# A two-layer decoder in float32: blocks of the retention stage between the products of the last projection, and accumulators that start from the residual

## Chip, cores, metric

One NeuronCore of a Trainium2 chip runs the whole program. The metric is the device time of one execution in microseconds (us); the number given for a kernel is the median of several executions. The engines are named as in the profile: PE is TensorE (matrix products), PEld its weight loads, DVE is VectorE, ACT is ScalarE, POOL is GpSimd, and SP is the engine that issues most of the transfers (DMAs). SPq and ACTq are the DMA queues of SP and ACT.

## The reference, cut to what matters

```python
h = concatenate([meta, x])                       # 16 + 1024 tokens, D_MODEL = 1024
h = h + mixer_rglru_swa(rmsnorm(h))              # layer 0
h = h + swiglu(rmsnorm(h))                       # (silu(h @ w_gate) * (h @ w_up)) @ w_down, D_FF = 2816
q, k, v, g = split(rmsnorm(h) @ w_in)            # layer 1: 4 heads, q and k 256 wide, v 512
for chunk in chunks_of_128(q, k, v):             # state: 256 x 512 per head
    qk = (qn @ kn.T) * decay_intra
    o = qk @ vn + (qn * decay_q) @ state
    state = decay_chunk * state + (kn * decay_k).T @ vn
h = h + (silu(g) * rmsnorm(o)) @ w_out
h = h + swiglu(rmsnorm(h))
return h[16:]                                    # everything in float32
```

## The kernel before, in words

Features lie on the partitions and tokens on the free axis, in two halves (`hf`). The stream `h` is eight tiles by two halves, `h[m][hf]`. A float32 product is three products of split operands (`mm3`, lines 160 to 162): each operand is written as a rounded part and a rest (`hi` and `lo` for a weight, `oh` and `ol` for an operand that moves). The rounded part is a cast on ACT (L111, L790), the rest a subtraction on DVE or POOL (L113, L791). The large products are done two tiles by two with seven products in place of eight: `unit22` loads four weight tiles and forms their sums and differences S1 to S4 on POOL (L145, L146, L149, L151), and `seven` runs the products in the order of `PRODUCTS` into two PSUM tags of four banks (`ps`, `ax`). After each product `evac` takes the result out of PSUM: a copy on ACT where a block of the output is met for the first time, else an add on DVE.

**The down projection of the FFN** (`ffn`, one per layer) goes over groups of two or three pairs of hidden tiles: `DG` has (2, 3, 2, 2, 2) pairs in layer 0 and (2, 3, 3, 3) in layer 1. The hidden tiles lie in DRAM (`hd`). Each group loads them again (seven tiles per pair, in `xslot`), splits them (`hilo` into `slot`), and runs four units `mp`, each of which adds into `h[2mp]` and `h[2mp+1]`. In group 0 the first product of a block writes a new tile `h` (ACT, L929), later products add (DVE, L840). The residual lies in DRAM too (`kept`): `residual(m)` loads two tiles after a unit of group 2 or 3 and adds them to `h[m]` on DVE (L910).

**The retention stage** follows the projections `proj7`. The last one, `proj7(15)`, is the gate's. Four heads have nine blocks each, `seq` is their list, and `turn(i)` runs block i: `updates` (six products for the state), `ahead(i + 2)` (load and split of the values with `values`, scores and key transposes with `first`), `outputs` (nine products) and `state` (DVE adds, ACT casts, DVE rests). `third` transposes a block's output and multiplies it with the gate `sg`, which `load_gates` fetches. When four blocks are through, their share of the output projection is put in `fills`, eight closures of twelve products, and `fill(n)` runs n of them. The blocks 0 to 2 of the first head are written ahead of `proj7(15)`; the rest of the loop opens a pool (`rp`) that takes over the memory of the projection's. The reloads of `h` stand in the turns 3 to 10.

The order on each engine is set by a scheduler: it takes the program's order as a priority and lets an instruction pass another one on the same engine when it expects the other to wait. Tiles come from pools: `slot` has 56 buffers, `xslot` 18, and a tile is handed out in the order of the program, when an earlier one is released. Each engine, and each DMA queue, then works strictly in its order.

## Time and profile before

| | |
|---|---|
| median of 3 executions | 2687.58 us (2685.81 to 2689.57) |
| the profiled execution: time, span | 2692.58 us, 2690.8 us |
| PE busy | 2583.9 us, 96% |
| DVE, ACT, POOL busy | 1828.1 us, 1157.2 us, 1454.5 us |
| mean granted clock of TensorE | 0.982 of full speed |
| DMA | 302.32 MB, mean 112 GB/s |

The span is the profiled execution from the first to the last instruction; its time lies 1.8 us above the span. A busy share near 100% of PE does not say that it runs at its peak: the ends of matmuls are modelled, and the granted clock has two levels, so a stretch with fewer matmuls per microsecond than its neighbours has lost time in either way.

### The profile page before, as it was taken

What the parts mean: (1) busy time and instruction counts of PE and PEld (TensorE: products, weight loads), DVE (VectorE), ACT (ScalarE), POOL (GpSimd) and SP (SyncE); (2) the same over time, 40 slices, a digit from 0 to 9 for tenths busy, and PEclk for the clock granted to TensorE, in tenths of its full rate; (3) what the DMA queues carried; (4) which work ended last, traced back from release to release, by engine and by line L of the source; (5) the groups of instructions that cost most, each with busy time, mean ns of one, the idle gap of its engine ahead of it and who ended that gap; (6) DMA issues with size and microseconds to landing.
All of it is one profiled execution on the core that took longest, in us unless ns stands there. A gap on an engine that the chain in (4) does not pass through costs nothing. (4 is left out here: it accounts for less than half of the span.)

```text
span 2690.8 us, 43341 instructions
## 1 busy us (share of the span) xinstructions
PE 2583.9 (96%) x15782; PEld 2289.4 (85%) x15782; DVE 1828.1 (68%) x3119; ACT 1157.2 (43%) x2452; POOL 1454.5 (54%) x1323
## 2 busy tenths in 40 slices
PE   8989999999999998999999998999999999998998
PEld 7878889999999898888999976777778888886776
DVE  6976677566666788987864434566688555556776
ACT  4665543333333533442233345555543333334542
POOL 4746143554554676456765444455555556544774
PEclk9998999999999999999999998999999999999999
DMA  4001152223223543332223234433332322323653
GB/s 153 30 27 37 55 177 78 96 96 112 91 96 135 186 155 108 118 118 103 95 101 98 96 126 160 147 112 126 127 128 90 111 99 98 106 98 118 208 170 112
DMA packets 145318, 302.32 MB, mean 112 GB/s; under 512 B 18512, under 2 KB 35408, under 8 KB 145104
## 3 DMA queue, kind: packets, MB, share of 16 engines
q1 hardware_dynamic: 103792, 232.49, 25.9%
q10 hardware_dynamic: 41152, 66.54, 6.6%
q8 instruction: 124, 2.03, 0.3%
q14 instruction: 90, 0.74, 0.1%
q0 software_dynamic: 160, 0.52, 0.1%
HBM read 216.60 MB, written 82.89 MB: 111 GB/s over the span
## 5 line engine op out<-in xcount | busy, mean ns | idle before, releaser
L160 PE MATMUL ps<-oh,hi 128*128 128x260 f32 (+1 forms) x2160 | 694.7, 324 | 25.9 <-DVE h L840 9.3
L161 PE MATMUL ps<-ol,hi 128*128 128x260 f32 (+1 forms) x2160 | 694.4, 322 | 5.1 <-POOL ol L791 2.8
L162 PE MATMUL ps<-oh,lo 128*128 128x260 f32 (+1 forms) x2160 | 691.4, 323 | 6.1 <-DVE lo L113 6.0
L160 PE MATMUL ax<-oh,hi 128*128 128x260 f32 (+1 forms) x1668 | 535.4, 323 | 5.4 <-DVE h L840 4.8
L161 PE MATMUL ax<-ol,hi 128*128 128x260 f32 (+1 forms) x1668 | 537.2, 323 | 2.3 <-DVE ol L791 1.6
L162 PE MATMUL ax<-oh,lo 128*128 128x260 f32 (+1 forms) x1668 | 532.8, 322 | 1.1 <-DVE lo L113 1.1
L113 DVE TENSOR_TENSOR lo<-S,hi 128x512 fp32r<-128x512 f32 (+2 forms) x380 | 332.5, 876 | 197.4 <-ACT hi L111 183.4
L160 PEld LDWEIGHTS ps<-oh,hi 128*128 128x128 f32 x2160 | 409.5, 190 | 65.1 <-DVE h L840 10.0
L162 PEld LDWEIGHTS ps<-oh,lo 128*128 128x128 f32 x2160 | 409.2, 190 | 41.6 <-DVE lo L113 9.5
L161 PEld LDWEIGHTS ps<-ol,hi 128*128 128x128 f32 x2160 | 410.8, 190 | 39.6 <-POOL ol L791 4.1
L111 ACT CAST hi<-S 128x512 fp32r<-128x512 f32 (+2 forms) x380 | 211.5, 559 | 526.8 <-PE ps L161 245.3
L160 PEld LDWEIGHTS ax<-oh,hi 128*128 128x128 f32 x1668 | 315.8, 190 | 32.0 <-DVE h L840 2.7
L161 PEld LDWEIGHTS ax<-ol,hi 128*128 128x128 f32 x1668 | 315.9, 189 | 28.8 <-DVE ol L791 2.7
L162 PEld LDWEIGHTS ax<-oh,lo 128*128 128x128 f32 x1668 | 314.3, 189 | 27.1 <-DVE lo L113 2.2
L299 POOL TENSOR_TENSOR t<-t,rf 128x520 f32<-128x520 f32 (+1 forms) x181 | 267.1, 1483 | 113.8 <-DVE t L1061 49.5
L111 ACT CAST hi<-raw 128x512 fp32r<-128x512 f32 (+2 forms) x350 | 202.6, 585 | 284.6 <-PE ps L161 142.4
L113 DVE TENSOR_TENSOR lo<-raw,hi 128x512 fp32r<-128x512 f32 (+2 forms) x318 | 258.0, 814 | 97.7 <-ACT hi L111 91.9
L145 POOL TENSOR_TENSOR S<-rb 128x512 f32<-128x512 f32 (+2 forms) x95 | 112.4, 1183 | 341.5 <-DVE lo L113 318.4
L791 POOL TENSOR_TENSOR ol<-raw,oh 128x520 fp32r<-128x520 f32 (+1 forms) x126 | 189.0, 1527 | 26.8 <-ACT oh L790 13.4
L151 POOL TENSOR_TENSOR S<-raw,S 128x512 f32<-128x512 f32 (+2 forms) x95 | 128.1, 1348 | 78.7 <-DVE lo L113 76.0
L146 POOL TENSOR_TENSOR S<-S,raw 128x512 f32<-128x512 f32 (+2 forms) x95 | 113.7, 1197 | 87.4 <-issue 46.3
L149 POOL TENSOR_TENSOR S<-raw,rb 128x512 f32<-128x512 f32 (+2 forms) x95 | 120.6, 1270 | 53.1 <-DVE lo L113 53.1
(306 smaller groups left out, 4812.3 us busy)
## 6 DMA issues: line engine op xcount, KB each, us to landing
raw<-in_wgu_dram SPq DMA_DIRECT2D x50, 512.0 KB, 3.3
raw<-hd SPq DMA_DIRECT2D x77, 260.0 KB, 4.3
raw<-hd SPq DMA_DIRECT2D x77, 256.0 KB, 3.4
rb<-in_wgu_dram SPq DMA_DIRECT2D x38, 512.0 KB, 3.2
raw<-in_wro_dram SPq DMA_DIRECT2D x32, 512.0 KB, 3.3
raw<-in_wr_dram SPq DMA_DIRECT2D x27, 512.0 KB, 3.3
hd<-T ACTq DMA_DIRECT2D x44, 260.0 KB, 2.6
hd<-T ACTq DMA_DIRECT2D x44, 256.0 KB, 3.9
```

The source lines that it names most:

```text
L111: nc.scalar.copy(hi, src)
L113: eng.tensor_tensor(out=lo, in0=src, in1=f32(hi), op=ALU.subtract)
L145: nc.gpsimd.tensor_tensor(out=s1, in0=a21, in1=a22, op=ALU.add)
L146: nc.gpsimd.tensor_tensor(out=s2, in0=s1, in1=a11, op=ALU.subtract)
L149: nc.gpsimd.tensor_tensor(out=s3, in0=a11, in1=a21, op=ALU.subtract)
L151: nc.gpsimd.tensor_tensor(out=s4, in0=a12, in1=s2, op=ALU.subtract)
L160: nc.tensor.matmul(ps, ah, bh, start=first and i == 0, stop=False, skip_group_check=more)
L161: nc.tensor.matmul(ps, ah, bl, start=False, stop=False, skip_group_check=more)
L162: nc.tensor.matmul(ps, al, bh, start=False, stop=last and i == n - 1, skip_group_check=more)
L299: (eng or nc.vector).tensor_tensor(out=out_, in0=a, in1=b, op=ALU.mult)
L791: eng.tensor_tensor(out=lo, in0=src, in1=f32(hi), op=ALU.subtract)
```

## The change

Four things are changed. `seven` takes hooks that run after a product. `proj7(15)` is called with hooks: after its first product the head of the sequence (`begin`), after the next six the turns 0 to 5; its temporaries come from `slot` rather than `aslot`. The values of a block are fetched three turns ahead (`fetch`) and no longer in `values`; the reloads of `h` are issued in the turns 3, 4, 6 and 7, four at a time, and `third` and `fill` are redistributed over the turns 6 to 9. In `ffn`, `preload` loads the residual into the tiles `h` of the units 1 to 3 ahead of their unit, so that all their products add on DVE and neither the copies on ACT nor a later residual add are left; the unit 0 keeps them (`residual(0)`, `residual(1)` in group 2). The rests of group 1's first pair go from DVE to POOL.

```diff
@@ -791,7 +791,7 @@
         eng.tensor_tensor(out=lo, in0=src, in1=f32(hi), op=ALU.subtract)
         return hi, lo
 
-    def seven(u, xs, chunks, evac):
+    def seven(u, xs, chunks, evac, hooks={}):
 
         bk = {}
         n = len(xs)
@@ -805,6 +805,8 @@
                                          xterm(x[xn_], a, b))], new and j == 0, j == n - 1,
                         not new)
             evac(i, [ps[:, :b - a] for ps, (a, b) in zip(bk[t], chunks)])
+            if i in hooks:
+                hooks[i]()
 
     def eight(u, xs, chunks, evac, hooks={}):
 
@@ -909,30 +911,39 @@
                 t = unspill(m, hf, n)
                 nc.vector.tensor_tensor(out=h[m][hf][:, :n], in0=h[m][hf][:, :n], in1=t[:, :n], op=ALU.add)
 
+        def preload(mp):
+            for m in (2 * mp, 2 * mp + 1):
+                for hf in range(2):
+                    h[m][hf] = unspill(m, hf, n, xslot if hf and m >= 4 else None)
+
         for gi, grp in enumerate(groups):
             xs = [{} for _ in grp]
             for ki, key in enumerate(MOVING):
                 for j, i in enumerate(grp):
                     raw = xslot("raw")[:, :n]
                     nc.sync.dma_start(raw, hd[i][key])
-                    xs[j][key] = hilo(raw, n, slot, nc.gpsimd if gi > 1 or j else nc.vector)
+                    xs[j][key] = hilo(raw, n, slot, nc.gpsimd if gi or j else nc.vector)
                 if gi == 0 and ki == 2:
                     keep()
+                if gi == 0 and ki == 4:
+                    preload(1)
             w = len(grp) * P
             for mp in range(4):
+                if gi == 0 and mp in (1, 2):
+                    preload(mp + 1)
                 at = [(2 * mp + r, c) for r, c in ((0, 0), (0, 0), (0, 1), (1, 1), (1, 1), (0, 1), (1, 0))]
 
                 def evac(k, bk):
                     m, hf = at[k]
-                    if gi == 0 and k in (0, 2, 3, 6):
+                    if gi == 0 and mp == 0 and k in (0, 2, 3, 6):
                         h[m][hf] = xslot("h") if hf and m >= 4 else slot("h")
                         each(lambda o, ps: nc.scalar.copy(o, ps), h[m][hf], bk)
                     else:
                         each(add, h[m][hf], bk, h[m][hf])
 
                 seven(unit22(wd[gi][mp], w, fp), xs, chunks, evac)
-                if gi in (2, 3):
-                    residual(4 * gi - 8 + mp)
+                if gi == 2 and mp in (1, 2):
+                    residual(mp - 1)
                 if gi == len(groups) - 1:
                     done(2 * mp)
                     done(2 * mp + 1)
@@ -1043,7 +1054,7 @@
             while pend:
                 pend.pop(0)()
 
-        def proj7(i, chunks, fin):
+        def proj7(i, chunks, fin, hooks={}):
             t = {}
 
             def evac(k, bk):
@@ -1064,7 +1075,7 @@
                 for f in held:
                     f()
 
-            seven(unit22(wr[i], 512, ap), xo2, chunks, evac)
+            seven(unit22(wr[i], 512, ap), xo2, chunks, evac, hooks)
 
         def scaled(chunks, c, t, bk):
             lo, hi = chunks[0][0], chunks[-1][1]
@@ -1185,6 +1196,7 @@
 
         def start(hd):
             k = Head()
+            k.raw = {}
             k.hd, k.kf, k.qf, k.kd, k.on, k.V, k.sp, k.ys, k.am, k.U, k.sg = hd, {}, {}, {}, {}, {}, {}, {}, {}, {}, {}
             return k
 
@@ -1201,11 +1213,20 @@
                     nc.sync.dma_start(k.kf[1][d][:, :512], k1[:, 8:520])
                     nc.sync.dma_start(k.qf[1][d][:, :512], q1)
 
+        def fetch(i):
+
+            if i >= len(seq):
+                return
+            k, b = seq[i]
+            if b in (0, 5):
+                load(k, b // 5)
+            k.raw = {b: slot("vr")[:, :512], **k.raw}
+            for p in range(2):
+                nc.sync.dma_start(k.raw[b][:block(b)[2], p * 256:(p + 1) * 256], vdr[k.hd][b][p])
+
         def values(k, b):
             bn = block(b)[2]
-            raw = slot("vr")[:, :512]
-            for p in range(2):
-                nc.sync.dma_start(raw[:bn, p * 256:(p + 1) * 256], vdr[k.hd][b][p])
+            raw = k.raw.pop(b)
             vh, vl = slot("vh", F32R)[:, :512], slot("vl", F32R)[:, :512]
             nc.scalar.copy(vh[:bn], raw[:bn])
             nc.gpsimd.tensor_tensor(out=vl[:bn], in0=raw[:bn], in1=f32(vh[:bn]), op=ALU.subtract)
@@ -1305,13 +1326,12 @@
 
             if i < len(seq):
                 k, b = seq[i]
-                if b in (0, 5):
-                    load(k, b // 5)
                 values(k, b)
                 first(k, b)
 
         def turn(i):
             k, b = seq[i]
+            fetch(i + 3)
             if b < 8:
                 updates(k, b)
             ahead(i + 2)
@@ -1320,12 +1340,24 @@
             if b < 8:
                 state(k, b)
 
-        ahead(0)
-        ahead(1)
+        def reload(ms, hf):
+            for m in ms:
+                h[m][hf] = unspill(m, hf, 512, rslot if hf else None)
+
+        def begin():
+            ahead(0)
+            ahead(1)
+
+        def hook(i):
+            def run():
+                turn(i)
+                if i in (3, 4):
+                    reload(range(4 * i - 12, 4 * i - 8), 0)
+            return run
+
         for i in range(3):
-            turn(i)
-        temps[0] = aslot
-        proj7(15, REST, gate(7))
+            fetch(i)
+        proj7(15, REST, gate(7), {0: begin, **{i + 1: hook(i) for i in range(6)}})
         while late_:
             late_.pop(0)()
 
@@ -1373,22 +1405,20 @@
             return [(lambda m=m: output(k.hd, hf, m, *k.ys[hf])) for m in range(KD)]
 
         for i, (k, b) in enumerate(seq):
-            if i > 2:
+            if i > 5:
                 turn(i)
-            if 3 <= i < 11:
-                for m in (2 * i - 6, 2 * i - 5):
-                    hf = m // KD
-                    h[m % KD][hf] = unspill(m % KD, hf, 512, rslot if hf else None)
+            if i in (6, 7):
+                reload(range(4 * i - 24, 4 * i - 20), 1)
             if b == 0:
-                fill(1)
-            for k_, b_ in seq[1:4] if i == 4 else seq[i - 1:i] if i > 4 else ():
+                fill(2 if i == 9 else 1)
+            for k_, b_ in {6: seq[1:3], 7: seq[3:5], 8: seq[5:8]}.get(i, seq[i - 1:i]) if i > 5 else ():
                 if not b_:
                     continue
                 third(k_, b_)
                 if b_ in (4, 8):
                     fills += outs(k_, b_ // 8)
             if i not in (32, 33, 34):
-                fill(1 if b in (0, 4, 5) else 2)
+                fill(3 if i < 9 else 1 if b in (0, 4, 5) else 2)
         fill(2)
         third(*seq[-1])
         fill(len(fills))
```

**SP, layer 0, behind the loads of group 0's hidden tiles.** `raw<-hd` is a hidden tile's load, `raw` and `rb<-in_wd` are a unit's weights, `h<-keep` is a residual's load. Before:

```order
L917 DMA raw_10703<-hd_6123 128x520
L141 DMA rb_11006<-in_wd_0_dram 128x512
L140 DMA raw_11153<-in_wd_0_dram 128x512
L141 DMA rb_11154<-in_wd_0_dram 128x512
L140 DMA raw_11427<-in_wd_1_dram 128x768
L141 DMA rb_11428<-in_wd_1_dram 128x768
L140 DMA raw_11613<-in_wd_1_dram 128x768
L141 DMA rb_11614<-in_wd_1_dram 128x768
L917 DMA raw_11301<-hd_6611 128x520
L140 DMA raw_11799<-in_wd_1_dram 128x768
```

and now:

```order
L924 DMA raw_10711<-hd_6123 128x520
L760 DMA h_10867<-keep_1913_4854 128x520
L760 DMA h_10871<-keep_1924_4901 128x520
L760 DMA h_11019<-keep_1935_4948 128x520
L760 DMA h_11023<-keep_1946_4995 128x520
L924 DMA raw_11313<-hd_6611 128x520
L924 DMA raw_11319<-hd_7111 128x520
L924 DMA raw_11325<-hd_7611 128x520
L924 DMA raw_11331<-hd_6613 128x520
L924 DMA raw_11337<-hd_7113 128x520
L141 DMA rb_11026<-in_wd_0_dram 128x512
```

The loads of group 1 (`hd_6611` is its first) stood behind the weights of group 1's second unit; now they stand ahead of the second half of the weights of group 0's unit 2, with the four residual loads of the units 2 and 3 ahead of them.

**POOL, the same place.** The rests of the hidden tiles are `ol<-raw,oh`; 128x256 sums belong to group 0, 128x384 ones to group 1. Before:

```order
L151 TENSOR_TENSOR S_11012<-raw_11005,S_11010 128x256
L151 TENSOR_TENSOR S_11160<-raw_11153,S_11158 128x256
L151 TENSOR_TENSOR S_11434<-raw_11427,S_11432 128x384
L145 TENSOR_TENSOR S_11617<-rb_11614 128x384
L146 TENSOR_TENSOR S_11618<-S_11617,raw_11613 128x384
L149 TENSOR_TENSOR S_11619<-raw_11613,rb_11614 128x384
L791 TENSOR_TENSOR ol_11310<-raw_11307,oh_11309 128x520
L151 TENSOR_TENSOR S_11620<-raw_11613,S_11618 128x384
```

and now:

```order
L151 TENSOR_TENSOR S_11032<-raw_11025,S_11030 128x256
L791 TENSOR_TENSOR ol_11316<-raw_11313,oh_11315 128x520
L145 TENSOR_TENSOR S_11173<-rb_11170 128x256
L791 TENSOR_TENSOR ol_11322<-raw_11319,oh_11321 128x520
L791 TENSOR_TENSOR ol_11328<-raw_11325,oh_11327 128x520
L791 TENSOR_TENSOR ol_11334<-raw_11331,oh_11333 128x520
L146 TENSOR_TENSOR S_11174<-S_11173,raw_11169 128x256
L791 TENSOR_TENSOR ol_11340<-raw_11337,oh_11339 128x520
L791 TENSOR_TENSOR ol_11346<-raw_11343,oh_11345 128x520
L791 TENSOR_TENSOR ol_11352<-raw_11349,oh_11351 128x520
L149 TENSOR_TENSOR S_11175<-raw_11169,rb_11170 128x256
L791 TENSOR_TENSOR ol_11358<-raw_11355,oh_11357 128x520
```

Seven rests of group 1 stand between the sums of group 0's last unit, where none stood, and all 21 of the group are now POOL's and stand ahead of the second sum (L146) of the group's second unit; before, POOL had 14 of the 21, one of them ahead of the second unit's last sum and 13 behind it.

**PE, the start of the first head.** `oh` and `ol` mark products of the projection, `kf` and `qf` the first transposes and scores of a block, `vh` and `kd` the update of the state. Before:

```order
L162 MATMUL ps_19484<-oh_14951,lo_19482 128x512
L1239 MATMUL ax_19612<-ckt,kf_19595 16x128
L1226 MATMUL ax_19625<-qf_19597,kf_19595 128x128
L1239 MATMUL ax_19638<-ckt,kf_19595 128x128
L1239 MATMUL ax_19638<-ckt,kf_19596 128x128
L1239 MATMUL ax_19612<-ckt,kf_19596 16x128
L1226 MATMUL ax_19625<-qf_19598,kf_19596 128x128
L160 MATMUL ax_19644<-vh_19608,kd_19615 128x512
L160 MATMUL ax_19648<-vh_19608,kd_19615 128x512
```

and now:

```order
L162 MATMUL ps_19460<-oh_14927,lo_19458 128x512
L1260 MATMUL ax_19651<-ckt,kf_19571 16x128
L1247 MATMUL ax_19661<-qf_19573,kf_19571 128x128
L1260 MATMUL ax_19674<-ckt,kf_19571 128x128
L160 MATMUL ax_19680<-oh_13770,hi_19602 128x512
...
L162 MATMUL ax_19680<-oh_14334,lo_19604 128x512
L1260 MATMUL ax_19674<-ckt,kf_19572 128x128
L1260 MATMUL ax_19651<-ckt,kf_19572 16x128
L1247 MATMUL ax_19661<-qf_19574,kf_19572 128x128
L160 MATMUL ps_19630<-oh_14691,hi_19608 128x512
...
L162 MATMUL ps_19630<-oh_14915,lo_19610 128x512
L160 MATMUL ax_19698<-vh_19647,kd_19654 128x512
```

Two of the last projection's products, twelve rows each (`ax_19680`, `ps_19630`), now stand between the first transposes and the first update, and its first product further ahead; before, the update came right behind the scores, and all seven products after it.

## Rows read from the trace of the kernel before

**Rows 1.** The page: busy time per engine (share of the span, instructions).

```profile
PE 2583.9 (96%) x15782; PEld 2289.4 (85%) x15782; DVE 1828.1 (68%) x3119; ACT 1157.2 (43%) x2452; POOL 1454.5 (54%) x1323
```

**Rows 2.** Stretches: length, busy us and instructions per engine, granted clock, DMA, GB/s.

```profile
1600.00:1720.00 120.00, 102.28 (x444) 80.64 (x443) 59.56 (x106) 61.17 (x136) 54.73 (x64) 0.91 0.46 155
1720.00:1840.00 120.00, 116.57 (x553) 93.98 (x552) 72.41 (x134) 64.51 (x147) 58.20 (x74) 1.00 0.39 132
910.00:930.00 20.00, 16.22 (x117) 14.40 (x116) 17.21 (x26) 14.26 (x27) 18.28 (x13) 1.00 1.00 356
930.00:985.00 55.00, 55.00 (x461) 55.00 (x460) 44.46 (x81) 23.74 (x47) 40.74 (x33) 1.00 0.53 164
985.00:1010.00 25.00, 21.84 (x152) 20.90 (x151) 24.22 (x45) 6.40 (x17) 20.80 (x19) 0.86 0.53 172
1030.00:1050.00 20.00, 12.77 (x72) 11.46 (x72) 18.50 (x30) 4.50 (x11) 14.41 (x12) 0.74 0.33 110
2480.00:2510.00 30.00, 25.48 (x91) 18.22 (x89) 19.26 (x26) 17.18 (x35) 19.20 (x16) 0.89 0.70 243
2520.00:2575.00 55.00, 55.00 (x239) 44.52 (x238) 39.84 (x55) 24.67 (x47) 45.33 (x35) 1.00 0.53 166
2575.00:2655.00 80.00, 74.83 (x312) 58.99 (x311) 67.32 (x86) 29.10 (x56) 61.86 (x46) 0.98 0.46 145
```

**Rows 3.** PE in order of time: start, length, what; in brackets idle time before, releaser.

```profile
1618.87 0.39 PE L162 MATMUL ps<-oh,lo 128*128 128x512 f32 x1
...
1626.89 1.30 PE L160 MATMUL ax<-vh,kd 16*128 16x512 f32 x2 [3.93 <-ACT kd L1243]
...
1669.70 1.47 PE L1293 MATMUL ax<-ckt,on 128*128 128x128 f32 x12
...
1692.50 0.62 PE L160 MATMUL ps<-yh,hi 128*128 128x512 f32 x1
```

**Rows 4.** SP's queue, 1587 to 1668 us, in order of time: start, length, what.

```profile
1657.84 8.21 SPq L122 DMA_DIRECT2D raw<-in_wro_dram  x2
...
1667.09 1.00 SPq L1208 DMA_DIRECT2D vr<-vd  x2
```

**Rows 5.** Waits of ACT, 1600 to 1720 us.

```profile
ACT vh L1210 <- DMA vr<-vd: 13.5, 4, 5.2
```

**Rows 6.** SP's queue in order of time, the loads of group 1 in either layer.

```profile
908.84 12.82 SPq L917 DMA_DIRECT2D raw<-hd  x19
...
2489.21 16.23 SPq L917 DMA_DIRECT2D raw<-hd  x21
```

**Rows 7.** ACT in order of time; in brackets its idle time before, and its releaser.

```profile
996.13 0.62 ACT L790 CAST oh<-raw 128x520 fp32r<-128x520 f32 x1 [6.71 <-DVE h L910]
...
1038.00 0.62 ACT L790 CAST oh<-raw 128x520 fp32r<-128x520 f32 x1 [5.29 <-DVE h L910]
```

**Rows 8.** Groups by line and shape: count, busy us, mean ns, idle before.

```profile
L791 POOL TENSOR_TENSOR ol<-raw,oh 128x520 fp32r<-128x520 f32 x63 | 93.9, 1515 | 8.9 <-PE ps L161 3.3 <-ACT oh L790 2.4 <-DVE h L840 2.3
L840 DVE TENSOR_TENSOR h<-ps,h 128x260 f32<-128x260 f32 x136 | 53.8, 419 | 15.2 <-PE ps L162 14.8
L910 DVE TENSOR_TENSOR h<-h,h 128x520 f32<-128x520 f32 x16 | 19.8, 1240 | 1.1 <-DMA h<-keep 1.1
L791 POOL TENSOR_TENSOR ol<-T,oh 128x520 fp32r<-128x520 f32 x8 | 16.8, 2106 | 26.4 <-ACT oh L790 26.4
```

**Rows 9.** POOL and ACT in order of time: last sums and last copies of group 0.

```profile
884.78 0.74 POOL L151 TENSOR_TENSOR S<-raw,S 128x256 f32<-128x256 f32 x1 [1.41 <-DVE lo L113]
...
912.47 0.38 ACT L929 COPY h<-ps 128x260 f32<-128x260 f32 x1 [0.28 <-PE ps L162]
...
2474.93 0.74 POOL L151 TENSOR_TENSOR S<-raw,S 128x256 f32<-128x256 f32 x1 [0.89 <-DVE lo L113]
...
2496.49 0.58 ACT L929 COPY h<-ps 128x512 f32<-128x512 f32 x1
```

**Rows 10.** DVE, the last instruction of the program.

```profile
2686.85 0.69 DVE L910 TENSOR_TENSOR h<-h,h 128x512 f32<-128x512 f32 x1
```

## The prediction, made before the run

> **What bounds the kernel now.** I read the page first. PE is busy for 2583.9 us, 96% of the span [rows 1], so work on another engine costs time only where PE waits for it or runs at the lower clock. Next I cut the span into stretches and looked for those with too few matmuls. The reader is to compare neighbours of one kind [rows 2]. In layer 0's down projection PE runs 461 matmuls in the 55 us from 930 on, 8.38 per us. From 910 to 930 it runs 117, worth 14.0 us, so 6.0 us are lost; from 985 to 1010 152, 6.9 lost; from 1030 to 1050 72, 11.4 lost: together 24.3 us. In layer 1 the clean stretch has 239 in 55 us, 4.35 per us; from 2480 to 2510 91 are worth 20.9 us, 9.1 lost; from 2575 to 2655 312 are worth 71.8, 8.2 lost: together 17.3 us. Around the start of the retention heads matmuls have several sizes, so I take idle time and clock: from 1600 to 1720 PE is idle for 17.7 us, and 102.3 busy us at a granted clock of 0.91 miss 9.2 us; the next 120 us, the same work in its steady state, miss 3.4. That is an excess of 23.5 us. The change touches these three places; together they have lost 65 us.
>
> Then I asked each place why. **The heads.** PE's matmuls of the last projection end at 1618.9, and the next large ones start at 1626.9, after a wait for a key tile (`kd`) of ACT's [rows 3]; the four blocks from 1669.7 to 1692.5 are as thin. ACT, which makes the key tiles, waits 13.5 us for values (`vr`) [rows 5], and key tiles queue behind that wait. The values are late since SP issues them late: those at 1667 right behind weight loads that SP held for 8.2 us [rows 4]. **The down projections, group 0 to group 1.** The hidden tiles of group 1 are issued from 908.8 and 2489.2 on [rows 6], when group 0 is almost over. Tiles of `xslot` are handed out in program order, and the last accumulators `h` of group 0 stand ahead of these loads. **Groups 2 and 3.** ACT stands for 6.7 and 5.3 us ahead of a cast whose buffer an L910 add holds [rows 7], and the casts of the next weights queue behind it.
>
> **The change, part by part.** *The residual as a start.* 24 of the 32 adds of L910 go, six pairs in either layer. An L910 of 520 columns takes 1240 ns, a PSUM add of 260 columns 419 ns [rows 8]. In place of 12 L910 per layer (14.9 us of DVE in layer 0) DVE gets 24 PSUM adds of 260 (10.1 us) which ACT's copies were. On paper that is little; what counts is the place: they go from groups 2 and 3, where DVE is at 24.2 of 25 and 18.5 of 20 us [rows 2], to group 0. The Trainium skill, "SBUF — State Buffer", section "Who interferes with whom", says why the one is dear: a DVE instruction with two SBUF inputs contends with GpSimd, one with at most one does not; the trace agrees, 1240 ns for twice the columns of a 419 ns add.
>
> With ACT's block gone I let 5 of the 6.9 us and 7 of the 11.4 us come back: not all, since POOL's bunches of splits between the sums stay, and the four remaining L910 now stand in group 2. Bounds: 0 and 18.3. In layer 1, 2575 to 2655, 4 of 8.2 (0 to 8.2). The end of the program was an L910 behind the last PSUM add [rows 10]; it falls away: 0.7 us, certain.
>
> *Group 1 earlier.* The twelve loads of the residual per layer are 3.2 MB; at the 356 GB/s of [rows 2] 9 us of DMA time, spread over group 0, in which DMA has room; by itself it costs nothing unless a weight comes late behind it. The gain is that splits of group 1 can start 40 us earlier, as far as `slot` has room: 56 buffers less 28 for group 0's operands and 12 accumulators leave 16, eight splits. But all 21 splits now run on POOL, at 1515 ns [rows 8]: 31.8 us, against 21.2 for 14 before. Layer 0: POOL is free at 885.5 [rows 9]; PE wants the last split at the seventh product of group 1's first unit: group 0's last block is copied out at 912.5 [rows 9], and six products of 18 matmuls at 8.38 per us are 12.9 us, so at 925.4, 39.9 us later. Demand: 31.8 and nine sums of 0.74 (256 columns) to about 1.0 us (384), 8: 39.8. Just met on paper; I leave 3 us of waiting in place of 6.0 and book 3 (bounds -6 and 6). Layer 1: free at 2475.7, wanted at 2496.5 [rows 9] + 6 x 9/4.35 = 2508.9, 33.2 us later; demand 31.8 and five sums, 36.8: 3.6 late, and more where the clock falls for it. Of 9.1 us I book 3 (bounds -6 and 9).
>
> A rule speaks against this edit. A rest takes POOL 1515 ns [rows 8], and seven more per layer load it with 10.6 us. The Trainium skill, "GPSIMD Engine Reference", section "Engine selection", wants elementwise work with two inputs on VectorE, GpSimd being about 2 times slower. By the rule alone, with POOL as the only engine that PE waits for at this crossing, all 10.6 would appear in either layer, and the sum would lose 21 us; the earlier start is what the rule leaves out.
>
> *Blocks between products.* No instruction of weight is added. Before, PE had nothing from 1618.9 to 1626.9 [rows 3] but a few transposes and scores. Now a product of 12 matmuls, 12/4.35 = 2.8 us, stands ahead of these and two stand behind: 8.3 us of cover for a hole of 8.0, after which the clock was low for a while. I book 9 for the two (bounds 5 and 10). What is next: the products run out by the fourth block, and blocks 3 to 8 then run without cover. A block has 15 large matmuls, 15/4.35 = 3.4 us, and some small ones: I take 4 us of PE. The values come one block earlier than before, but the `sg` loads and the twelve reloads of `h` share SP with them: from the first reload to the fourth `sg` there are about 5.9 MB, at 356 GB/s 16.6 us, and `third` needs all four. I leave 10 us of loss here and in the start together: 23.5 - 10 = 13.5 gained (bounds -5 and 20).
>
> *The later heads.* Values are fetched three turns ahead rather than two. The stretch from 1720 misses 3.4 us only [rows 2]: nothing booked, 0 to 3.
>
> **The sum.** 5 + 7 + 4 + 0.7 + 3 + 3 + 13.5 = 36.2 us. The profiled execution took 2692.6 us, so 2656.4 for it. The median of the runs is 5.0 lower than that execution: 2651.4, rounded to 2652.
>
> **The rivals.**
> *The first head starves.* The products are used up early, `third` waits for `sg`, and PE idles at blocks 4 to 8. For: the queue just counted, and four blocks without cover took 22.8 us from 1669.7 to 1692.5 before [rows 3], 5.7 each, 1.7 more than PE's work; for 5.5 blocks 9.4, and half clock with it. Against: the values are there earlier. The heads gain nothing: 2652 + 13.5 = 2665.5; with 8 us lost besides, 2674.
> *GpSimd takes over the crossing, slower than before.* Splits of group 1 do not start early, because the loads or their buffers come late, and POOL binds. From the start of group 0's last unit to the end of group 1's first PE has 84 + 126 matmuls in layer 0, 25 us (layer 1: 24), POOL 31.8 and 10 of sums: 17 lost per layer, not 3 and 6: 25 more, 2677. From a price per rest of 1515 + (2687.6 - 2677)/42 = 1770 ns on it decides the sign: at the 2106 ns of the rests of `T` [rows 8], 42 x 0.59 = 25 us more, 2702. For: those 2106 ns, measured while DVE worked beside it. Against: DVE no longer splits there, and 12 of 21 rests stand ahead of the sums in the new order.
> *Nothing comes of it.* Hidden waits swap places, as at 1.8 us per rest above: 2683 to 2692.
> *More comes back.* All three places recover three quarters or more of their 65 us: 2652 - 18 = 2634 and below.
>
> **Numbers.** Forecast (2640 to 2664) 0.56; starving (2664 to 2677) 0.16; nothing, or GpSimd just short of the sign (2677 to 2693) 0.10; slower by GpSimd 0.05; more (under 2640) 0.13. The range 2632 to 2677 leaves out about 0.2: 0.15 above, half of "more" below. What a measurement of this kernel can tell is 0.2%, 5.4 us. Faster by more than that 0.88, within 0.06, slower 0.06.
>
> **What would show it.** After the change: the hidden loads of group 1 from about 870 and 2455 on; no loss left at 1030 to 1050; L910 8 times; POOL at or near full from the start of group 0's last unit through group 1's first, with PE's waits there naming POOL's `ol`, about 3 and 6 us; no wait of ACT for `vr` over 3 us; PE busy from 1619 to 1650, and its waits of the first head moved to blocks 4 to 8, for `yt` or `kd`. I am wrong if PE's matmul rate in group 1's first unit falls below 6 per us, or if the first head's unfilled blocks take over 7 us each.

## The result, and the profile after

The changed kernel takes 2658.34 us (median of 4 runs, 2653.24 to 2662.21) against 2687.6: ratio 0.9890, 95% interval 0.9868 to 0.9912, or 24 to 36 us less. The forecast was 2652, within 2632 to 2677. The profiled execution has a span of 2653.1 us, 37.7 under the one of before.

The page of the changed kernel, busy time per engine, beside [rows 1]:

```profile
PE 2566.4 (97%) x15782; PEld 2277.6 (86%) x15782; DVE 1820.0 (69%) x3117; ACT 1142.6 (43%) x2416; POOL 1468.4 (55%) x1337
```

The same stretches as in [rows 2] (length, busy us and instructions of PE, PEld, DVE, ACT, POOL, granted clock, DMA, GB/s):

```profile
1600.00:1720.00 120.00, 112.60 (x504) 89.14 (x503) 71.76 (x127) 69.35 (x160) 66.47 (x79) 0.93 0.51 172
910.00:930.00 20.00, 19.52 (x159) 19.01 (x158) 15.88 (x31) 7.36 (x15) 20.00 (x15) 1.00 0.65 193
985.00:1010.00 25.00, 22.64 (x179) 21.55 (x178) 24.93 (x51) 7.69 (x19) 20.36 (x20) 1.00 0.45 136
1030.00:1050.00 20.00, 19.22 (x160) 19.02 (x159) 17.31 (x44) 5.62 (x14) 12.49 (x14) 1.00 0.20 66
2480.00:2510.00 30.00, 28.57 (x118) 22.21 (x117) 19.95 (x29) 8.44 (x17) 18.25 (x17) 0.97 0.37 112
2575.00:2655.00 80.00, 74.14 (x320) 59.70 (x318) 47.58 (x68) 23.97 (x46) 42.90 (x33) 0.98 0.28 94
```

The reader is to see more matmuls in each: 160 for 72 from 1030 on, 159 for 117 from 910, 118 for 91 from 2480, 504 for 444 in the first head. The last stretch ends with the program, at 2653.1.

But such windows slide: after the change the same work lies earlier in them. Both traces hold 15,782 matmuls, so the times can be compared at equal work. I give each matmul the spacing that its kind has in clean stretches (0.120 us for 260 columns, 0.2325 for 512, 0.118 for 256, 0.122 for 264, about 0.11 for the small ones), which sums to 2504 us, and read how much more time each kernel takes from one amount of work to the next. That excess, idle time and low clock alike, is the table; the stages are cut at the same work in all (in brackets, where they begin in the trace of before). Between the first stage and the second every kernel loses 0.8 us, which is left out. "The crossing" is below the stage from group 0 to group 1. Columns as named below.

```
us lost in              before after again  e1    e2    e3    e5    e11   e6    e7    e10   e12
first 260 us of work     66.3  61.7  61.3  62.4  59.7  59.9  62.2  62.0  62.0  62.2  61.3  61.8
layer 0, start (863)      9.0  14.5  14.6  14.8   9.0  12.2   9.0   9.9  16.0  15.4  11.8  10.3
  group 0 to 1 (886)      6.3   2.6   2.5   2.6   7.4   7.9   7.6   2.0   2.6   2.5   2.3   8.1
  group 1 to 2 (963)      7.1   3.8   3.7   3.7   6.4   3.8   6.4   6.3   3.8   3.8   4.0   4.0
  group 2 to 3 (1020)    11.5   1.0   1.0   1.0  11.5   1.0  11.5  11.7   1.0   1.0   0.7   0.7
  to the heads (1071)    12.1  10.0  10.1   9.3  12.3  10.0  12.3  11.6  10.0   9.2   9.2  10.5
first head (1599)        29.4  17.9  17.6  27.1  20.1  19.0  18.4  18.6  31.2  29.4  18.3  21.6
later heads (1743)       10.5   9.7   9.6  10.3   9.3   9.6   9.4   9.9  11.5  10.0   9.6  11.3
layer 1, start (2427)    11.8  13.3  12.4  11.9  12.0  12.6  12.1  11.9  12.0  12.2  13.5  19.1
  group 0 to 1 (2485)     9.2   6.8   6.8   5.8   8.7  11.4  10.7   5.2   5.6   6.9   6.8   2.1
  later groups (2534)     7.7   2.7   5.4   4.1   7.2   2.4   6.0   8.6   3.8   2.7   1.6   4.2
end                       5.3   4.6   4.6   4.6   5.3   4.6   5.3   5.3   5.0   4.5   4.6   4.6
```

Layer 0's down projection and what follows it gave 14.1 us (46.0 to 31.9), the first head 11.5, the later heads 0.8, layer 1's down projection 5.9 and the end 0.7. The other 4.6 us lie in the first 260 us of work, which the change doesn't touch; the profiled execution of before was 5.0 us above its median. Two profiles of the changed kernel (`after`, `again`) agree within 1 us in every stage but the last groups of layer 1 (2.7). A column is one execution each, and kernels whose code for a stage is the same scatter more: the first head loses 17.6 to 21.6 us in those that have all of the new head. A difference below 4 us there is not read.

### The profile page after: what moved, and what is told of

The parts are those of the page before. It is cut to its first block, busy times and chain, and to the rows that moved or that the text cites. A ratio compares the mean times of both kernels' runs of the same rounds, so it can differ in the third digit from the quotient of the medians.

```text
span 2653.1 us, 43334 instructions
## 1 busy us (share of the span) xinstructions
PE 2566.4 (97%) x15782; PEld 2277.6 (86%) x15782; DVE 1820.0 (69%) x3117; ACT 1142.6 (43%) x2416; POOL 1468.4 (55%) x1337
## 4 chain that ended last, share of the span: by engine, by line
PE 80%; DVE 10%; ACT 3%; issue 3%; POOL 2%; DMA 2%; SPq 0%; DVEq 0%; ACTq 0%; POOLq 0%
PE ps L160 16%; PE ps L162 16%; PE ps L161 16%; PE ax L160 9%; PE ax L161 9%; PE ax L162 9%; DVE lo L113 2%; POOL ol L791 1%; DVE ol L791 1%; DVE h L842 1%; DVE xp L770 1%; PE ps L681 1%; DVE T L785 1%; PE ps L1147 1%; DVE qs L299 0%
## 5 line engine op out<-in xcount | busy, mean ns | idle before, releaser
L113 DVE TENSOR_TENSOR lo<-raw,hi 128x512 fp32r<-128x512 f32 (+2 forms) x318 | 270.2, 853 | 95.6 <-ACT hi L111 90.4
L791 POOL TENSOR_TENSOR ol<-raw,oh 128x520 fp32r<-128x520 f32 (+1 forms) x140 | 202.5, 1473 | 33.2 <-ACT oh L790 14.4
L146 POOL TENSOR_TENSOR S<-S,raw 128x512 f32<-128x512 f32 (+2 forms) x95 | 112.7, 1186 | 85.7 <-issue 46.3
```

Of the source, the lines that this page charges most:

```text
L113: eng.tensor_tensor(out=lo, in0=src, in1=f32(hi), op=ALU.subtract)
L146: nc.gpsimd.tensor_tensor(out=s2, in0=s1, in1=a11, op=ALU.subtract)
L791: eng.tensor_tensor(out=lo, in0=src, in1=f32(hi), op=ALU.subtract)
```

## The experiments

**The two halves by themselves, and the changed kernel again.** e1 takes only `ffn` from the changed kernel, e2 all but `ffn`.

> The kernel before with the edits of the down projections alone (residual as a start, group 1's rests on POOL); the heads stand as before. Theory A, each stage loses what PE waits for in that stage and the parts add up: at equal work of PE the profiled executions part by 14.3 us in layer 0's down projection, 5.9 in layer 1's and 0.75 at the end, 20.9 in all, so 2687.6 - 20.9 = 2667 (2663 to 2671). Rival, the parts share their gain (what one frees the other would have freed too, or a gain in one place is given back later): under 2662 or over 2673.

> The changed kernel with the down projections as before; only the retention stage is changed. Theory A: 11.6 us at the start of the first head, so 2687.6 - 11.6 = 2676 (2672 to 2680), and nothing moved in the down projections. Rival: the later order of the reloads and the gates changes layer 1's down projection too, or the gain needs both: outside 2672 to 2680.

> The changed kernel once more, as a measure of what a run of the same program varies by: 2658 (2653 to 2662), and by stage the losses within 1 us of the first profile, but for the first 260 us, where the profiles of one and the same code were 6 us apart.

Measured: e1 2664.33 us (ratio 0.9901, 0.9886 to 0.9916), e2 2680.06 (0.9959, 0.9943 to 0.9975), again 2656.25 (0.9880, 0.9865 to 0.9894). e1 lies in the range of its theory A; e2 lies at the upper edge of its own (2680), in a round in which the kernel before took 2690.2, and by its ratio it is 2676.6. In the table e1 has the new losses in the down projections and 27.1 us in the first head, e2 the reverse. The product of the two ratios, 0.986, lies 0.002 to 0.003 under the changed kernel's, about what the intervals leave open. The parts add up by stage; that they do so to the last 6 us of the medians is not shown.

**Is it the early loads or the early residual?** e5 allocates the accumulators early, but loads no residual into them; ACT copies and late adds stand as before. e11 also writes one column of each where it is allocated.

```diff
 def preload(mp):
-    h[m][hf] = unspill(m, hf, n, xslot if hf and m >= 4 else None)
+    h[m][hf] = xslot("h") if hf and m >= 4 else slot("h")           # e5 and e11
+    nc.vector.tensor_copy(h[m][hf][:, :1], ident[:, :1])            # e11 only
...
-if gi == 0 and mp == 0 and k in (0, 2, 3, 6):
+if gi == 0 and k in (0, 2, 3, 6):
...
-if gi == 2 and mp in (1, 2): residual(mp - 1)
+if gi in (2, 3): residual(4 * gi - 8 + mp)
```

> The changed kernel with the residual added late again: the accumulators of units 1 to 3 are allocated where the change loads them, but nothing is loaded; group 0's first products are copied out by ACT and L-numbers of the residual add run in groups 2 and 3 as before. What stays of the change in the down projections is the earlier loads of group 1 and all its rests on POOL. Theory A, the two edits act in different places: the crossing from group 0 to 1 keeps its gain (3.7 us in layer 0, 2.4 in layer 1), the gains of groups 2 to 4 (3.3 + 10.5 + 4.5 us in layer 0, 5 in layer 1) and of the end (0.7) go, and the start of group 0 is as before (5.5 and 1.6 us back): 2658 + 17 = 2675. Rival, the earlier loads alone thin out the later groups as well (their splits are done sooner, so the adds have room): 2656 to 2666.

> The run e5_late_residual with one edit: each accumulator of the units 1 to 3 gets one column written by a small DVE copy at the place of its allocation, so that its buffer is handed out there and the loads of group 1's hidden tiles (from 865 us on, before 905) no longer stand behind the last copy of group 0. No residual is loaded early. Theory B, early loads make the gain of the crossing: layer 0's crossing falls from 7.6 us lost to 2 to 4, layer 1's from 10.7 to 6 to 8, the later groups stay as in e5 (6.4 + 11.5 + 7.1 us in layer 0); 2677 - 8 = 2669. At the start of group 0 the loads of group 1 alone fill the DMA engines or not: 9 us lost if the residual's loads are to blame, 12 to 15 if group 1's are. Rival, the crossing needs ACT free of the copies: it stays at 7 and 10 us lost, 2675 to 2679.

Measured: e5 2677.13 us (0.9950, 0.9935 to 0.9965), e11 2669.97 (0.9930, 0.9913 to 0.9947). e5 met its total and missed a part: the crossing kept nothing (7.6 and 10.7 us lost). SP's queue of e5 says why: allocating a tile did not hand its buffer on, and the loads of group 1 stayed where they were.

```profile
904.77 12.53 SPq L924 DMA_DIRECT2D raw<-hd  x17
```

In e11 the written column hands it on, and group 1's loads follow group 0's directly (the first 10 of these are group 0's, the others group 1's; in the kernel before, over 40 us lay between the two):

```profile
850.78 16.23 SPq L925 DMA_DIRECT2D raw<-hd  x14
...
867.53 6.45 SPq L925 DMA_DIRECT2D raw<-hd  x7
```

Now the crossings lose 2.0 and 5.2 us, and the later groups of layer 0 as much as before (6.3 and 11.7). So the crossings gain nothing without the early loads, the gain of layer 0's later groups comes of the residual as a start, and e11's start of group 0 (9.9 for 9.0) says that group 1's early loads cost little there. e3, below, shows that the early loads alone are not enough at the crossings either.

**What the start of group 0 loses.** The changed kernel lost 5.5 us more than before there, which I had booked at nothing. e4 moves the calls for unit 1's four residual loads behind those for all hidden tiles. e10 holds the residual of the units 2 and 3 back until unit 0's first accumulator is out, e12 that of all three.

```diff
 def unspill(m, hf, n=512, pool=None, behind=None):
     t = pool("h") if pool else slot("h")
+    if behind is not None:                                          # e10: mp > 1; e12: all
+        nc.vector.tensor_copy(t[:, :1], behind[:, :1])              # behind = h[0][0]
...
-if gi == 0 and ki == 4: preload(1)                                  # e4, e12
+if gi == 0: preload(1)        # e4: ahead of unit 0; e12: with preload(2), ahead of unit 1
```

> The changed kernel with the first four loads of the residual (unit 1's) issued behind group 0's hidden loads and no longer between them. Theory A, the start of group 0 loses 5.5 us more than before in layer 0 and 1.6 in layer 1 because hidden loads stand behind four loads that wait 4.9 us for a buffer in SP's queue: both come back, 2658 - 7 = 2651. Rival, the volume of the 12 loads, not their place in the queue, delays the hidden tiles and the weights: no change, 2656 to 2661.

> The changed kernel with the residual loads of the units 2 and 3 held back: one column of each of these tiles is first written by a small DVE copy of unit 0's first accumulator, so that the loads cannot start before group 0's first products are out. (The unit 1's four loads stay.) Theory A, the start of group 0 loses 5.5 us more than before because these loads and those of group 1's hidden tiles fill the DMA engines (busy share 0.93 for 0.47) while the last hidden tiles are stored and loaded: the start falls from 14.5 to about 10 us in layer 0 and from 13.4 to 12 in layer 1, 2658 - 5 = 2653. Rival, it is not the volume but the new order on ACT and the clock that falls with the first wait: the start stays at 14 to 15 and 2656 to 2661 is measured.

> As e10_hold, but all twelve residual loads of a layer are held back, unit 1's too: they are issued after group 0's first products are copied out, behind all hidden loads of the group. Theory B, the residual's loads at the start of group 0 are what it loses there (14.5 us with them, 11.8 with unit 1's four alone, 9.0 to 9.9 with none): the start falls to 9 to 10 us in layer 0, the crossing stays at 2 to 3, the groups 2 and 3 at 4 and 1; 2657 - 7 = 2650, ratio to the kernel before 0.985. Rival, the unit 1's first adds now wait for their residual and the loss moves there: the start stays at 11 to 12 or the crossing rises by 2 to 4, 2653 to 2658.

Measured: e4 2658.75 us (0.9878, 0.9862 to 0.9895), e10 2652.61 (0.9858, 0.9843 to 0.9872), e12 2662.93 (0.9893, 0.9877 to 0.9908). e4's start still loses 14.9 us, but e4 does not test its theory. The first four residual loads in SP's queue are not unit 1's. They are one half each of the units 2 and 3 (in the order of the program, shown with the change, they come in two pairs): these tiles come from `xslot`, where 14 hidden tiles of group 0 and these four fill the 18 buffers. They stand behind all hidden loads of group 0 in the changed kernel already (at 858.12, for 4.85 us, 3.2 of them a wait for earlier loads to land, not for a buffer), and e4 leaves them there:

```profile
848.64 7.45 SPq L924 DMA_DIRECT2D raw<-hd  x10
856.19 4.67 SPq L760 DMA_DIRECT2D h<-keep  x4
```

Unit 1's four follow at 872.6 in the changed kernel and at 874.1 in e4. e10 is the run that takes the first four away. Its start loses 11.8 us, e12's 10.3. Two stretches at the start, first the kernel before, then the changed one, then e10:

```profile
855.00:865.00 10.00, 8.78 (x74) 8.57 (x72) 6.62 (x14) 1.90 (x5) 2.96 (x3) 1.00 0.84 270
865.00:875.00 10.00, 7.25 (x39) 6.39 (x40) 8.95 (x10) 6.84 (x13) 7.84 (x6) 0.83 0.61 211
```

```profile
855.00:865.00 10.00, 6.03 (x43) 5.40 (x42) 6.22 (x12) 2.06 (x4) 3.03 (x4) 0.95 0.98 321
865.00:875.00 10.00, 7.89 (x42) 6.93 (x41) 7.71 (x7) 5.53 (x11) 7.18 (x5) 0.71 1.05 394
```

```profile
855.00:865.00 10.00, 6.94 (x48) 6.29 (x48) 8.36 (x13) 4.00 (x8) 5.04 (x5) 0.92 1.00 342
865.00:875.00 10.00, 7.09 (x46) 6.33 (x45) 9.49 (x13) 6.73 (x16) 7.39 (x7) 0.84 0.58 185
```

The DMA engines are full for 20 us in the changed kernel, for 10 in e10; but in the first 10 they are as full in e10 (1.00 for 0.98). ACT, which stores the last hidden tiles (`hd<-T`) and casts the first loaded ones, shows what the four loads do. The kernel before:

```profile
864.29 1.09 ACTq L902 DMA_DIRECT2D hd<-T  x2
865.42 0.62 ACT L790 CAST oh<-raw 128x520 fp32r<-128x520 f32 x1 [1.01 <-DVE t L299]
...
867.07 1.68 ACT L790 CAST oh<-raw 128x520 fp32r<-128x520 f32 x3
```

The changed kernel, whose time there is 4.5 us earlier:

```profile
859.77 2.52 ACTq L904 DMA_DIRECT2D hd<-T  x2
862.33 0.62 ACT L790 CAST oh<-raw 128x520 fp32r<-128x520 f32 x1 [2.44 <-DMA raw<-hd]
...
865.48 2.21 ACT L790 CAST oh<-raw 128x520 fp32r<-128x520 f32 x4 [0.83 <-DMA h<-keep]
```

And e10:

```profile
859.33 0.96 ACTq L906 DMA_DIRECT2D hd<-T  x2
860.33 0.62 ACT L792 CAST oh<-raw 128x520 fp32r<-128x520 f32 x1 [0.88 <-DVE t L299]
```

The two stores take 2.52 us in place of 1.09. Each is 0.33 us long, but the second starts only at 861.97. The landings in the trace say what it waits for. SP and ACT share eight semaphores that tell of a landing, and their transfers use them in turn. In the traces of the kernel before, of the changed one (both profiles) and of e10, none of some 1000 transfers starts before the last one on its semaphore has landed, so no more than eight are under way. The four residual loads take four of the eight. So the second store starts 0.08 us after a hidden tile's load has landed (861.89), the next at 863.65, 0.07 after another (863.58), and the last at 865.11, 0.07 after the first residual load (865.04); the casts stand behind these stores. In the kernel before and in e10 no store follows such a landing so closely.

Counted from ACT's weight cast just before (864.00 and 859.49), the first three of these casts come 1.4, 2.1 and 2.9 us later than before here, and 0.4, 1.5 and 1.6 us in the second profile, which loses as much (14.6). PE waits for them and then runs longer at the lower clock (0.71 for 0.83 in the second stretch). All profiles agree: in the eight with four residual loads there, the two stores take 1.50 to 2.60 us, PE is idle for 7.1 to 9.1 us in this stage and 12.2 to 16.0 are lost; in the six without (before, e2, e5, e10, e11, e12) it is 0.94 to 1.09, 5.1 to 6.1 and 9.0 to 11.8. What e10 still loses over before is clock: PE is idle for 6.1 us (6.0 before), but at the lower clock for 10.2 (3.4 before); why stays open. In layer 1 e10 gives nothing (13.5 us lost for 13.3), and ACT's two stores take 1.26 us with such loads and without, so the small loss there has no cause shown.

e12 went too far: unit 1's first adds come before their residual. DVE, in order of time:

```profile
889.81 0.76 DVE L844 TENSOR_TENSOR h<-ps,h 128x260 f32<-128x260 f32 x2 [2.40 <-DMA h<-keep]
```

The loss moved there (8.1 us at layer 0's crossing, 19.1 at layer 1's start). e10 is the fastest kernel measured here, with a span 4.8 us under the changed kernel's; its ratio lies under both of the changed kernel's, with intervals that overlap at the edge, so that it is better is likely and not settled.

**Seven rests more on GpSimd.** e3 gives group 1's first pair back to DVE.

```diff
-xs[j][key] = hilo(raw, n, slot, nc.gpsimd if gi or j else nc.vector)
+xs[j][key] = hilo(raw, n, slot, nc.gpsimd if gi > 1 or j else nc.vector)
```

> The changed kernel with the rests of group 1's first pair back on DVE (7 of 21 per layer). Theory A, POOL's order holds the sums back at the crossing from group 0 to 1 (PE loses some 2.8 us there in layer 0 and 6.7 in layer 1, waiting for lo of sums that stand behind runs of rests): POOL is freed of 7 x 1.45 = 10 us per layer and the loss falls, 2658 - 5 = 2653. Rival, the place on DVE costs what POOL gives: DVE's rests come between PSUM adds, the two engines contend, 2657 to 2666 and waits of PE for DVE in place of POOL.

Measured: 2666.00 us (0.9913, 0.9897 to 0.9930). Theory A falls: the crossings lose 7.9 and 11.4 us for 2.6 and 6.8. PE's longest wait of e3 from 885 to 965 us (total, times, longest), then DVE's rests from 880 to 960:

```profile
PE ps L160 <- DVE h L842: 3.8, 2, 2.5
```

```profile
L791 DVE TENSOR_TENSOR ol<-raw,oh 128x520 fp32r<-128x520 f32 x7 | 7.3, 1039 | 0.0
```

In the changed kernel POOL's 23 rests of the same stretch take 1448 ns each:

```profile
L791 POOL TENSOR_TENSOR ol<-raw,oh 128x520 fp32r<-128x520 f32 x23 | 32.7, 1448 | 3.1 <-DMA rb<-in_wd_dram 3.1
```

The reader is to see that a rest is cheaper on DVE, 1039 ns for 1448, and dearer where it stands: between the PSUM adds (`h`), for which PE then waits. The Trainium skill, "GPSIMD Engine Reference", section "Engine selection", puts elementwise work on VectorE, since GpSimd is about 2 times slower with two inputs; the ratio here is 1.4, and the trace doesn't agree with the choice: moving the rests by that rule cost 5.3 + 4.6 = 9.9 us at the crossings. By the ratios it is some 6 to 9 us, with intervals that still touch one of the two of the changed kernel. The crossings of e3 lose more than before (6.3 and 9.2), though its loads are early: the gain there needs both the early loads and the rests on POOL, and neither alone gives any.

**Cover or early values?** e6 loads the values where they are split, as before (`fetch(i)` in `ahead`, none ahead of it). e7 keeps `fetch` and puts the seven products in one block behind turn 2.

```diff
-proj7(15, REST, gate(7), {0: begin, **{i + 1: hook(i) for i in range(6)}})
+begin()                                                             # e7
+for i in range(3): hook(i)()
+proj7(15, REST, gate(7))
+for i in range(3, 6): hook(i)()
```

> The changed kernel with the values of a block loaded where they are split, as before, and no longer three turns ahead; the products still stand between the blocks. Theory A, the cover by the products makes the gain of the first head and late values hide behind it: 2658 to 2662, ACT's waits for vr up to 13 us again but PE busy. Rival, the early values make the gain: 2665 or more, PE waiting for kd and sh behind ACT's wait for vr, and losses in the later heads too.

> The changed kernel with the products of the last projection in one block again, behind the first three turns as before; the values are fetched ahead and the reloads stand where the change puts them (turns 3 to 5 come right behind the projection). Theory A: the 7 us gained in the first stretch of the head are lost again and blocks 3 to 5, now without cover too, stay as they are: 2658 + 7 = 2665. Rival, the early values make the gain: 2656 to 2661.

Measured: e6 2672.59 us (0.9932, 0.9909 to 0.9956), e7 2666.54 (0.9913, 0.9899 to 0.9928). e7 met theory A's number, but by stage it lost 11.5 us in the first head, not 7; e6 is its rival's case. The first head loses 29.4 us before, 31.2 with the products between but late values, 29.4 with early values but no products between, 17.9 with both: taking either edit away costs the whole gain. Both runs keep the new places of the reloads, of `third` and of `fill`; what these cost or give by themselves was not run. In e6 the cover lasts until it is used up, and then ACT stands for values with the state's cast `sh` behind it. Waits of e6 (ACT from 1600 to 1720, PE from 1655 to 1680):

```profile
ACT vh L1231 <- DMA vr<-vd: 7.8, 4, 5.6
```

```profile
PE ps L160 <- ACT sh L302: 5.0, 1, 5.0
```

In e7 the hole at the head's start is there again, PE in order of time:

```profile
1606.99 1.30 PE L160 MATMUL ax<-vh,kd 16*128 16x512 f32 x2 [2.18 <-ACT kd L1264]
```

**The blocks without cover.** e8 moves the second half of the reloads of `h` behind the calls of `third` in the turns 6 and 7.

> The changed kernel with the second half of the reloads of h behind the third calls of turns 6 and 7, so that all four sg loads and the key tiles of the second head stand ahead of them in SP's queue. Theory A, the 8.8 us lost between 1657 and 1670 begin with DVE's waits for sg (7.3 us) and PE's for yt and kf (5 us): 3 to 6 us come back, 2658 - 4 = 2654. Rival, the blocks without cover are bound by their own chain (ACT on, DVE ss, yt, ACT yh) and the loads only hide it: 2656 to 2660, the waits for sg gone and others in their place.

Measured: 2661.58 us (0.9899, 0.9872 to 0.9926): no change. Waits from 1600 to 1680 of the changed kernel, then of e8:

```profile
DVE yt L299 <- DMA sg<-gd: 7.3, 2, 4.8
...
PE ax L1314 <- DVE yt L299: 3.3, 2, 2.4
```

```profile
DVE yt L299 <- DMA sg<-gd: 3.8, 1, 3.8
...
PE ax L1314 <- DVE yt L299: 2.9, 1, 2.9
```

The wait for the gates halves, PE's wait for `yt` hardly changes, PE now waits 2.2 us for `kd` as well, and the first head loses 17.4 us for 17.9. What binds these blocks, about 9 us from 1655 to 1670, stays open: their own chain is the rival that the run leaves, and it was not tried apart.

## Why the prediction was right, step by step

The likeliest case came true, within its own range: 36.2 us were summed, 33 are in the changed stages by the table and 29 in the medians. That the sum is so close is in part luck, as the terms show:

- *Groups 2 and 3 of layer 0*, 5 and 7 booked: 3.3 and 10.5, and 2.1 behind them that I had not booked; *layer 1's later groups*, 4 booked: 5.0, or 2.3 by the second profile. e1, e5 and e11 show the cause: nearly all of layer 0's part goes with the late adds (e5 and e11 keep 0.7 and 0.8 of the 3.3, and none of the 10.5); layer 1's scatters too much to say. L910 (now L912) runs 8 times, 4 in each layer:

```profile
L912 DVE TENSOR_TENSOR h<-h,h x8: 682/1076/1499, 981.3 to 2555.9; 128x520 f32<-128x520 f32 x4, 128x512 f32<-128x512 f32 x4
...
  ACT oh L790: 10.7, 2
```

  Of my two reasons, ACT's block and DVE's load, the traces bear out the second more. Before, PE's longest waits from 1000 to 1100 name DVE's adds out of PSUM:

```profile
PE ps L160 <- DVE h L840: 5.8, 4, 1.7
PE ax L160 <- DVE h L840: 2.4, 1, 2.4
```

  A weight behind ACT's block is named once, for 1.3 us at 997.7. After the change the waits for adds from 980 to 1080 are 2.2 us, though ACT still stands behind two late adds for 10.7 us (last line of the view above). One of the two, 6.2 us for 6.7 before, lies in group 2, where the loss fell from 7.1 to 3.8.

- *The end*, 0.7 booked: 0.7.
- *The crossings*, 3 and 3 booked: 3.7 and 2.4. The hidden tiles of group 1 are issued from 865.4 and 2418.2 us on. The stages begin 4.5 and 31.1 us earlier than before, so at equal work this is 870 and 2449, about the 870 and 2455 that I had said. SP's queue (window from 820, then from 2405):

```profile
858.12 4.85 SPq L760 DMA_DIRECT2D h<-keep  x4
865.42 3.52 SPq L924 DMA_DIRECT2D raw<-hd  x5
...
2418.22 3.73 SPq L924 DMA_DIRECT2D raw<-hd  x5
```

POOL is full there, 20.0 of 20 us from 910. I had counted the seven more rests on POOL as the price of the early loads; e3 shows that they are part of the gain. The remaining losses of 2.6 and 6.8 us have the size that I gave (3 and 6), but PE's waits do not name `ol` for 3 and 6 us. In layer 0, from 890 to 960, they are 1.4 us in all:

```profile
PE ps L160 <- DVE h L842: 0.9, 1, 0.9
PE ps L161 <- POOL ol L791: 0.5, 2, 0.3
```

  In layer 1 they name `lo`: a sum stands behind a run of rests, and DVE's `lo` of that sum and of the weights behind it are late. That is read from the order, not tried. POOL in order of time, and PE's waits from 2440 to 2520:

```profile
2462.85 9.79 POOL L791 TENSOR_TENSOR ol<-raw,oh 128x512 fp32r<-128x512 f32 x7
2472.61 1.01 POOL L151 TENSOR_TENSOR S<-raw,S 128x384 f32<-128x384 f32 x1
```

```profile
PE ps L162 <- DVE lo L113: 3.3, 3, 1.8
...
PE ps L161 <- POOL ol L791: 0.2, 1, 0.2
```

- The rival *GpSimd takes over the crossing* was run as e5, where the loads come late and POOL has all 21 rests. It priced 17 us lost per layer; measured are 7.6 and 10.7, only 1.3 and 1.5 above before. A rest took 1448 ns, not over 1770: it can't decide the sign here.
- *The twelve loads of the residual*, booked at nothing "unless a weight comes late behind it", is the step that failed: 5.5 us in layer 0 and 1.5 in layer 1 (0.6 by the second profile). I had spread 9 us of transfers over group 0 and looked only for weights behind them. Four of the twelve are issued at the moment when the last hidden tiles go out and come in, since `xslot` has room for them, and what is late is not a weight but ACT's stores, which wait for earlier transfers to land, and the casts behind the stores. e10 and e12 show that the loads at that moment cost part of it (14.5 to 11.8 and 10.3 us); the way through ACT is read from the landings, and the rest is clock. Layer 1's part stays open.
- *The first head*, 13.5 booked: 11.5. The hole is filled (the longest wait of PE at the start is 0.8 us, at 1613), ACT's waits for `vr` are 5.2 us in all, the longest 2.8, for 13.5 and 5.2, and PE's waits moved to the blocks without cover, as said. My reason was incomplete: I gave the gain to the cover and little to the values, and e6 and e7 show that it takes both. *The later heads*, 0 booked: 0.8. PE at the head's start, and ACT's waits for values from 1600 to 1720:

```profile
1613.13 0.79 PE L160 MATMUL ax<-vh,kd 128*128 128x512 f32 x1 [0.82 <-DVE am L299]
```

```profile
ACT vh L1231 <- DMA vr<-vd: 5.2, 3, 2.8
```

The errors nearly cancel, and nothing in the working made them do so: 7.0 us lost at the starts of group 0 and 2.0 less in the first head, against 3.9 more in layer 0's later groups, 1.0 in layer 1's and 0.8 in the later heads.

## What to carry to other kernels

A load that is moved early is not free because its queue is idle: it takes one of the places for transfers under way, so ask which stores and loads come behind it in those 10 us, and tie it to the first result that makes it useful, but not later than its first reader. An operation that is faster on one engine can still belong on the slower one, when it would stand in the first engine's queue between what the bottleneck waits for. Two edits can give nothing alone and much together, as at the crossings and, as far as it was run, in the first head, so test them together and apart before calling one the cause. And look in the trace at what an edit moved before reading its time: e4 left the loads that mattered where they were.

## What the runs showed of the hardware that was not expected

An engine that issues a transfer can wait for another engine's. The pair of stores on ACT took 2.52 us (1.50 in the second profile) where SP had put four more loads among the eight transfers that can be under way here, and 0.96 in e10 without these loads, though the DMA share of those 10 us was 1.00 for 0.98. The share does not tell it; the landings do, and ACT's casts wait behind its stores. The eight belong to this program, which gives SP's and ACT's transfers eight semaphores; no run has another number.

The first 260 us of work, the same code in all kernels, lost 59.7 to 62.4 us in thirteen profiles and 66.3 in that of before. Differences of 5 us between single executions therefore need a comparison by stage.
